# One head's first attention pass alternated with another head's second pass

## The chip, the cores and the metric

The kernel runs on one core of a Trainium2 chip. The metric is the device time of one execution in microseconds (us). The core has five engines with queues of their own: TensorE (PE, matmuls), VectorE (DVE), ScalarE (ACT), GpSimd (POOL) and SyncE (SP, which here only issues DMAs). Each engine takes its instructions in the order that was fixed when the program was compiled.

## The reference

One layer of a hybrid encoder over 2048 positions with 1024 channels, in float32. Cut to what matters here:

```python
def forgetting_attention(q, k, v, f_logit):           # 8 heads of 64, blocks of 128 queries
    c = jnp.cumsum(jax.nn.log_sigmoid(f_logit), axis=1)
    s = jnp.einsum('bhtd,bshd->bhts', qi, k) * Dh ** -0.5
    s = s + ci[..., :, None] - c[:, :, None, :]
    s = jnp.where(kpos[None, :] <= qpos[:, None], s, -jnp.inf)
    p = jax.nn.softmax(s, axis=-1)
    return jnp.einsum('bhts,bshd->bthd', p, v)

h = rms_norm(x, norm_mix_g);  z = h @ w_in
out_a = spatial_gating(gelu(u), gelu(v), ...)         # 8 gating heads
out_b = forgetting_attention(q, k, v, f)              # 8 attention heads
x = x + concat(out_a, out_b) @ w_out
x = x + conv_ffn(rms_norm(x, norm_ffn_g), w_up, w_conv, b_conv, w_down)
return rms_norm(x, norm_final_g)
```

The feed-forward part projects up to 2 x 2816 channels, applies a causal convolution of width 3, a SiLU gate, and projects down.

## The kernel before

**Main work.** The 2048 positions are taken in two halves of 1024, and each half in two token blocks of 512. A float32 matmul is made of three matmuls on rounded high and low parts: `mm3` (L206 to L214; the matmul itself is L212) does so for the projections. `a_half` does the input projections and the gating heads, `c_half` the output projection of the first half, `d_half` the up-projection and convolution of the first half in 22 slices of 128 channels (`d_up`, four times 24 matmuls of 512 columns per slice), `c_late` the output projection of the second half, and `late_half` the rest. In `d_up` a result leaves PSUM by two ACT operations (L934, L935); DVE then does the halo copies (L936, L937), the taps (L938, L939), the gate (L947) and the product (L950). Weights are loaded raw, cast to a high part on POOL (L151), and the low part is made on DVE (L165). In every second slice `d_sums` combines rows of the down-projection on POOL (L992).

**Attention.** A piece is one head and one block `tb` of 512 queries; there are 32, eight heads for each of the four blocks. A piece has two passes over its `tb + 1` blocks of 512 keys:

- `b_max`, the first pass, finds for each query the largest score: for a key block and 128 queries, one matmul into a score bank (L777) and one DVE reduction (L780, or L782 with the causal mask). That is one unit; a piece with `tb` = 3 has 16.
- `b_mix`, the second pass, takes 128 keys a unit: two matmuls for the transposed scores (L824, L828; L826 adds the mask), `Exp` on ACT (L830), a rounded copy on ACT (L835), the low part on DVE (L836), the running sum of the weights on DVE (L838), and, three units later, two matmuls with the values into the output bank (L812, L813). At its end the sums are turned (L854) and, for each pair of heads, the result is scaled and written to the DRAM tensors `mixh` and `mixl`.

The row maxima of the first pass go into rows 96 to 104 of the piece's query tile `t1` by `turn()` (L796, L797).

**Tiles.** `b_keys` (L743) loads key tiles: `m1` (136 KB, wanted by both passes), and for the second pass `m2` and the values `v`. `self.M1` is a ring of two `m1` tiles whose constant rows are set once (L702); both passes take turns in it. `t1` has two buffers, the second query tile `t2` (loaded by `b_low`) and the sum tile `sum` have one each. Behind the first two slices of `d_half`, `self.more` is set and the pool `bxpool` is opened: `room` (L729) then takes tiles `e`, `ph`, `pl`, `m2`, `v` from additional buffers too (names with a `+`), and `scores` (L736) takes two banks named `dn` beside the three named `s`.

**Order.** `b_stream` (L708) yields once per unit. `tick` calls one step of it for every `rate` main matmuls (3.6 in `d_half` and `c_late`). The program so traced is ordered for each engine at compile time by priority: earlier in the program first, with the steps of the stream set 100 instructions ahead (`AHEAD_B`) and weight preparation 2000 (`AHEAD_W`). An instruction that isn't ready is passed by those behind it. `need(n)` finishes the stream up to block `n` at points where its result is read: `c_late` needs block 3 behind its first column of the first token block, and then loads `mixh` and `mixl` of that block (`load_mix`, L872) for its second token block.

In `b_stream` the first pass of a piece runs in full, then the second pass of the piece before it:

Of the kernel before, what the change touches and what calls it, by code (L numbers as in the profile page):

```python
# [8 lines left out]
F32 = mybir.dt.float32  # L9
F32R = mybir.dt.float32r  # L10
# [8 lines left out]
P = 128  # L19
# [6 lines left out]
TB = 512  # L26
# [7 lines left out]
AHEAD_B, AHEAD_W = 100, 2000  # L34
WARM = 24
LAG = 2
TURN = 3
GATE_LAG = 30

# [14 lines left out]
def f32(ap):  # L54
    return ap.bitcast(F32)
# [26 lines left out]
class Block:  # L82
# [625 lines left out]
    def b_stream(self, pieces):  # L708

        todo = None  # L710
        for h, tb in pieces:
            if tb >= 2 and not self.ready:
                if todo:
                    yield from self.b_mix(*todo, None)
                    self.done += 1
                    todo = None
                while not self.ready:
                    yield
            t1, turn = yield from self.b_max(h, tb)
            if todo:  # L720
                yield from self.b_mix(*todo, turn)
                self.done += 1
            else:
                turn()
            todo = (h, tb, t1, self.b_low(h, tb))
        yield from self.b_mix(*todo, None)
        self.done += 1

    def room(self, shape, dt, tag):  # L729

        n = self.nroom[tag] = self.nroom.get(tag, -1) + 1
        if self.more and n % (BUFS[tag] + BUFS[tag + "+"]) >= BUFS[tag]:
            return self.til(self.bx, shape, dt, tag + "+")
        return self.til(self.bp if tag == "e" else self.mp, shape, dt, tag)
# [7 lines left out]

    def b_keys(self, h, sb, values):  # L743
        hf, sl = sb // 2, slice((sb % 2) * TB, (sb % 2 + 1) * TB)
        self.M1.append(self.M1.pop(0))
        m1 = self.M1[0]
        self.dma(f32(m1[0:68, :]), self.kx[hf][h, 64:132, sl])
        if not values:
            return m1
        m2 = self.room([P, TB], F32R, "m2")  # L750
        self.dma(f32(m2), self.kx[hf][h, 0:128, sl])
        v = self.room([P, 4, P], F32R, "v")
        self.dma(f32(v), self.vd[hf][sl, h, :].rearrange("(c p) d -> p c d", p=P))
        return m1, m2, v

    def b_low(self, h, tb):

        t2 = self.til(self.mp, [P, TB], F32R, "t2")
        self.dma(f32(t2), self.qx[tb // 2][h, :, (tb % 2) * TB:(tb % 2 + 1) * TB])
        return t2  # L760

# [37 lines left out]

        return t1, turn  # L800

    def b_mix(self, h, tb, t1, t2, turn):

        nc, bp, pp = self.nc, self.bp, self.bpp
        po = self.til(pp, [P, TB], F32, "o")
        total = self.til(self.mp, [P, TB], F32, "sum")
        ns = 4 * tb + 4
        late = []

        def pv():  # L810
            sc, c, v, ph, pl = late.pop(0)
            nc.tensor.matmul(po[:, c], lhsT=v, rhs=ph[:, c], start=sc == 0, stop=False)  # L812
            nc.tensor.matmul(po[:, c], lhsT=v, rhs=pl[:, c], start=False, stop=sc == ns - 1)  # L813

        for sc in range(ns):
            if sc == TURN and turn:
                turn()
            if sc % 4 == 0:
                m1, m2, v4 = self.b_keys(h, sc // 4, True)
            j = max(0, sc - 4 * tb)  # L820
            c = slice(j * P, TB)
            ks = slice((sc % 4) * P, (sc % 4 + 1) * P)
            ps = self.scores([P, TB])
            nc.tensor.matmul(ps[:, c], lhsT=m1[:, ks], rhs=t1[:, c], start=True, stop=False)  # L824
            if sc >= 4 * tb:
                nc.tensor.matmul(ps[:, j * P:(j + 1) * P], lhsT=self.same, rhs=self.maskT, start=False, stop=False,  # L826
                                 skip_group_check=True)
            nc.tensor.matmul(ps[:, c], lhsT=m2[:, ks], rhs=t2[:, c], start=False, stop=True)  # L828
            e = self.room([P, TB], F32, "e") if sc else total
            nc.scalar.activation(e[:, c], ps[:, c], AF.Exp, scale=-1.0)  # L830
            if len(late) >= (LAG + 1 if self.more else LAG):
                pv()
            ph = self.room([P, TB], F32R, "ph")
            pl = self.room([P, TB], F32R, "pl")
            nc.scalar.activation(ph[:, c], e[:, c], AF.Copy)  # L835
            nc.vector.tensor_tensor(pl[:, c], e[:, c], f32(ph[:, c]), op=ALU.subtract)  # L836
            if sc:
                nc.vector.tensor_tensor(total[:, c], total[:, c], e[:, c], op=ALU.add)  # L838
            late.append((sc, c, v4[:, sc % 4, :], ph, pl))
            yield  # L840
        while late:
            pv()
            yield

        if h % 2 == 0:
            self.op = self.til(self.mp, [P, TB], F32, "op")
            self.rr = self.til(bp, [P, 4, 2], F32, "rr")
        op = self.op
        own, other = (slice(0, 64), slice(64, 128)) if h % 2 == 0 else (slice(64, 128), slice(0, 64))
        nc.scalar.activation(op[own, :], po[other, :], AF.Copy)  # L850
        nc.vector.tensor_tensor(op[own, :], po[own, :], op[own, :], op=ALU.add)
        ps = self.scores([P, 4])
        for i in range(4):
            nc.tensor.matmul(ps[:, i:i + 1], lhsT=total[:, i * P:(i + 1) * P], rhs=self.mhalf[:, 0:1], start=True, stop=True)  # L854
        nc.vector.reciprocal(self.rr[:, :, h % 2], ps)
        if h % 2 == 0:
            return

        rw = self.til(self.mp, [P, 4, 2, 64], F32, "rw")
        nc.scalar.activation(rw, self.rr.unsqueeze(3).broadcast_to([P, 4, 2, 64]), AF.Copy, scale=-0.5)  # L860
        yield
        pr = self.transpose4(None, "s", [rw[:, i, :, :].rearrange("p a b -> p (a b)") for i in range(4)])
        nc.vector.tensor_tensor(op, pr, op, op=ALU.mult)
        oh = self.room([P, TB], F32R, "ph")
        ol = self.room([P, TB], F32R, "pl")
        self.split_sb(op, oh, ol)
        cs = slice(512 + (h - 1) * 64, 512 + (h + 1) * 64)
        self.dma(self.mixh[tb][cs, :], f32(oh))
        self.dma(self.mixl[tb][cs, :], f32(ol))
# [84 lines left out]
    def d_half(self):  # L954

        units = lambda f: [self.load_unit(self.a["w_up"][c], P) for c in (f, NF + f)]
        for f0 in range(0, NF, 2):
# [17 lines left out]
            if not f0:  # L975
                self.flush()
                self.accs.close()
                self.bx = self.bxs.enter_context(self.tc.tile_pool(name="bxpool", bufs=1, side="right", reuse_waits="tile"))
                self.more = True
    def d_sums(self, i):  # L980

        nc, dp = self.nc, self.dp
# [579 lines left out]
```

## Time and profile before

| | |
|---|---|
| median of three runs | 2421.57 us (2420.01 to 2422.13) |
| the profiled execution's own time | 2422.66 us |
| its span in the trace | 2420.9 us |
| granted PE clock, mean | 0.995 |
| first unit that uses the additional score banks | 967.5 us |
| last value matmul of attention (L813) | 1512.5 us |

How to read it: busy times are unions of an engine's instructions. Matmuls are pipelined, so that one of 512 columns is shown as 390 ns long while the next starts 226 ns behind it; the pace of PE is read from starts and counts, not from durations. In rows of waits and timelines, "<-" names what ended the wait. Tile names stand without buffer numbers, so `m` is `m1` or `m2`, and `t` is `t1` or `t2`, or the convolution's `t`.

### The profile page before, as it was taken

How to read it: one execution, taken by the hardware profiler on the slowest of the kernel's cores; microseconds unless marked ns; L12 is line 12 of the kernel's file. 1: busy time of each engine (PE TensorE's matmuls, PEld its weight loads, DVE VectorE, ACT ScalarE, POOL GpSimd, SP SyncE). 2: the span in 40 equal slices, each digit the busy share in tenths (PEclk: the TensorE clock that was granted, in tenths of full speed). 3: DMA queues.
4: the chain of work that ended last, by engine and by line, in shares of the span. 5: the costliest groups of instructions: out<-in, count | busy, mean ns of one | idle time of the engine just before them, and what ended most of it. 6: DMA issues, size and time to landing. Idle time of an engine off the chain costs nothing.

```text
span 2420.9 us, 32633 instructions
## 1 busy us (share of the span) xinstructions
PE 2379.3 (98%) x11352; PEld 1973.2 (82%) x11352; DVE 1881.9 (78%) x3196; ACT 1152.9 (48%) x1987; POOL 331.3 (14%) x315
## 2 busy tenths in 40 slices
PE   9999999999999999999999999899999999999998
PEld 7888878988787888888878888688888888888887
DVE  5457776776579888998999988598888877857775
ACT  4335655533334444454544445465555455454444
POOL 4014140010232222222221110100000000000001
PEclk9999999999999999999999999899999999999999
DMA  8662625567754444444443464312222228438633
GB/s 278 184 230 94 197 74 171 153 188 247 244 193 151 154 142 153 147 140 158 160 155 121 159 217 152 122 53 95 79 81 85 87 93 313 159 98 296 205 119 123
DMA packets 234518, 379.58 MB, mean 157 GB/s; under 512 B 49944, under 2 KB 109464, under 8 KB 232928
## 3 DMA queue, kind: packets, MB, share of 16 engines
q1 hardware_dynamic: 229312, 353.36, 44.9%
q0 software_dynamic: 5040, 24.12, 2.6%
q8 instruction: 90, 1.47, 0.3%
q14 instruction: 76, 0.62, 0.1%
HBM read 283.82 MB, written 93.72 MB: 156 GB/s over the span
## 4 chain that ended last, share of the span: by engine, by line
PE 79%; DVE 5%; DMA 2%; issue 2%; ACT 2%; POOL 1%; SPq 0%; POOLq 0%; DVEq 0%; ACTq 0%
PE mm L212 35%; PE D L1376 13%; PE A L1174 3%; PE A L1176 3%; PE A L1175 3%; PE o L813 3%; PE o L812 2%; PE s L777 2%; PE s L828 2%; PE s L824 2%; PE B L1175 2%; PE B L1176 2%; PE B L1174 2%; PE C L1174 1%; PE C L1175 1%
## 5 line engine op out<-in xcount | busy, mean ns | idle before, releaser
L212 PE MATMUL mm<-thi,wlo 128*128 128x512 f32 x896 | 352.9, 394 | 0.0
L212 PE MATMUL mm<-thi,whi 128*128 128x512 f32 x896 | 352.1, 393 | 0.5 <-DVE vn L520 0.5
L212 PE MATMUL mm<-tlo,whi 128*128 128x512 f32 x896 | 352.5, 393 | 0.0
L212 PE MATMUL mm<-whi,thi 128*128 128x512 f32 (+2 forms) x768 | 277.4, 362 | 14.3 <-DMA thi<-mixh 8.8
L212 PE MATMUL mm<-wlo,thi 128*128 128x512 f32 (+2 forms) x768 | 276.7, 361 | 1.9 <-DVE wlo L165 1.8
L212 PE MATMUL mm<-whi,tlo 128*128 128x512 f32 (+2 forms) x768 | 275.4, 360 | 1.3 <-DMA tlo<-mixl 1.3
L151 POOL TENSOR_SCALAR whi<-raw 128x1024 fp32r<-128x1024 f32 (+3 forms) x114 | 135.2, 1187 | 909.3 <-PE mm L212 665.9
L212 PEld LDWEIGHTS mm<-thi,whi 128*128 128x128 f32 x896 | 168.8, 188 | 34.5 <-issue 0.9
L212 PEld LDWEIGHTS mm<-tlo,whi 128*128 128x128 f32 x896 | 168.8, 188 | 33.9
L212 PEld LDWEIGHTS mm<-thi,wlo 128*128 128x128 f32 x896 | 168.9, 188 | 33.2
L838 DVE TENSOR_TENSOR sum<-sum,e 128x512 f32<-128x512 f32 (+3 forms) x249 | 163.6, 657 | 20.8 <-ACT e L830 18.2
L212 PEld LDWEIGHTS mm<-whi,thi 128*128 128x128 f32 x768 | 146.1, 190 | 35.8 <-DMA thi<-mixh 9.6
L212 PEld LDWEIGHTS mm<-wlo,thi 128*128 128x128 f32 x768 | 146.1, 190 | 22.5 <-DVE wlo L165 3.1
L212 PEld LDWEIGHTS mm<-whi,tlo 128*128 128x128 f32 x768 | 146.0, 190 | 21.4 <-DMA tlo<-mixl 1.7
L830 ACT ACTIVATE e<-s 128x512 f32<-128x512 f32 (+3 forms) x207 | 105.9, 518 | 114.0 <-PE s L828 64.1
L165 DVE TENSOR_TENSOR wlo<-raw,whi 128x1024 fp32r<-128x1024 f32 (+2 forms) x106 | 134.8, 1274 | 28.0 <-POOL whi L151 27.6
L1376 PE MATMUL D<-wh,xh 128*128 128x512 f32 x368 | 140.8, 389 | 1.2 <-DVE xo L1477 1.2
L1376 PE MATMUL D<-wl,xh 128*128 128x512 f32 x368 | 141.4, 389 | 0.0
L836 DVE TENSOR_TENSOR pl<-e,ph 128x512 fp32r<-128x512 f32 (+3 forms) x195 | 122.2, 632 | 20.5 <-PE o L813 10.7
L1376 PE MATMUL D<-wh,xl 128*128 128x512 f32 x368 | 137.5, 389 | 0.0
L835 ACT ACTIVATE ph<-e 128x512 fp32r<-128x512 f32 (+3 forms) x195 | 104.4, 547 | 42.4 <-PE o L812 29.5
L934 ACT ACTIVATE a<-mm 128x512 f32<-128x512 f32 x88 | 52.4, 596 | 119.5 <-PE mm L212 119.1
(1839 smaller groups left out, 5776.2 us busy)
## 6 DMA issues: line engine op xcount, KB each, us to landing
raw<-in_w_up_dram SPq DMA_DIRECT2D x72, 512.0 KB
m<-kx SPq DMA_DIRECT2D x160, 136.0 KB
x<-act SPq DMA_DIRECT2D x84, 256.0 KB
m<-kx SPq DMA_DIRECT2D x67, 256.0 KB
v<-vd SPq DMA_DIRECT2D x67, 256.0 KB
raw<-in_w_in_dram SPq DMA_DIRECT2D x28, 512.0 KB
raw<-in_w_out_dram SPq DMA_DIRECT2D x24, 512.0 KB
tw<-in_w_down_dram SPq DMA_DIRECT2D x11, 1024.0 KB
```

The costliest lines, as they stand in the source:

```text
L151: self.cast_ins = self.nc.gpsimd.tensor_scalar(out, in_, 1.0, 0.0, ALU.mult, ALU.add).ins
L165: nc.vector.tensor_tensor(lo, raw, f32(hi), op=ALU.subtract)
L212: self.last_mm = self.nc.tensor.matmul(ps, lhsT=a[k], rhs=b[k], start=i == 0, stop=i == 3 * n - 1).ins
L813: nc.tensor.matmul(po[:, c], lhsT=v, rhs=pl[:, c], start=False, stop=sc == ns - 1)
L830: nc.scalar.activation(e[:, c], ps[:, c], AF.Exp, scale=-1.0)
L835: nc.scalar.activation(ph[:, c], e[:, c], AF.Copy)
L836: nc.vector.tensor_tensor(pl[:, c], e[:, c], f32(ph[:, c]), op=ALU.subtract)
L838: nc.vector.tensor_tensor(total[:, c], total[:, c], e[:, c], op=ALU.add)
L1174: mm(ps, lhsT=xh[:, ks], rhs=yh[:, k, :], start=fresh and k == 0, stop=False, **kw)
L1175: mm(ps, lhsT=xh[:, ks], rhs=yl[:, k, :], start=False, stop=False, **kw)
L1176: mm(ps, lhsT=xl[:, ks], rhs=yh[:, k, :], start=False, stop=k == 3, **kw)
L1376: nc.tensor.matmul(bank[t], lhsT=x[i][:, ts], rhs=w[k], start=fresh and j == 0 and i + k == 0, stop=last and i == 1, **kw)
```

## The change

While `self.more` holds, three units of the new piece's first pass alternate with two units of the second pass of the piece before, until the first pass is done; the rest of the second pass follows, and `turn()` is called behind its fourth unit. The second pass gets a ring of its own of two key tiles, `self.M1b`, whose constant rows are set by four memsets on POOL when `bxpool` is opened. `t2` and `sum` get a second buffer each, and `t2` is loaded at the start of the second pass, not at the end of the round before.

```diff
+FIRST, SECOND = 3, 2
...
-    ... "m2+": 1, "v+": 1,
+    ... "m2+": 1, "v+": 1, "m1+": 2, "sum+": 1, "t2+": 1,
...
-            t1, turn = yield from self.b_max(h, tb)
-            if todo:
-                yield from self.b_mix(*todo, turn)
+            if todo and self.more:
+                first, second = self.b_max(h, tb), self.b_mix(*todo, None)
+                t1 = None
+                while t1 is None:
+                    for _ in range(FIRST):
+                        t1, turn = yield from self.one(first)
+                        if t1 is not None:
+                            break
+                    if t1 is None:
+                        for _ in range(SECOND):
+                            yield from self.one(second)
+                for n, _ in enumerate(second):
+                    if n == TURN:
+                        turn()
+                        turn = None
+                    yield
+                if turn:
+                    turn()
                 self.done += 1
             else:
-                turn()
-            todo = (h, tb, t1, self.b_low(h, tb))
+                t1, turn = yield from self.b_max(h, tb)
+                if todo:
+                    yield from self.b_mix(*todo, turn)
+                    self.done += 1
+                else:
+                    turn()
+            todo = (h, tb, t1)
...
+    def one(self, gen):
+        try:
+            next(gen)
+        except StopIteration as end:
+            return end.value or (None, None)
+        yield
+        return None, None
...
     def b_keys(self, h, sb, values):
-        self.M1.append(self.M1.pop(0))
-        m1 = self.M1[0]
+        ring = self.M1b if values and self.more else self.M1
+        ring.append(ring.pop(0))
+        m1 = ring[0]
...
     def b_low(self, h, tb):
-        t2 = self.til(self.mp, [P, TB], F32R, "t2")
+        t2 = self.room([P, TB], F32R, "t2")
...
-    def b_mix(self, h, tb, t1, t2, turn):
+    def b_mix(self, h, tb, t1, turn):
+        t2 = self.b_low(h, tb)
         po = self.til(pp, [P, TB], F32, "o")
-        total = self.til(self.mp, [P, TB], F32, "sum")
+        total = self.room([P, TB], F32, "sum")
...
                 self.more = True
+                self.M1b = [self.til(self.bx, [P, TB], F32R, "m1+") for _ in range(2)]
+                for m in self.M1b:
+                    self.nc.gpsimd.memset(f32(m[64:128, :]), 0.0)
+                    self.nc.gpsimd.memset(f32(m[96:104, :]), 1.0)
```

2 rows, old and new, of the table BUFS are left out of this document.

## The prediction, as it stood before the changed kernel was run

> **What bounds the kernel now.** I read the page first, then busy time by stretches, then the waits and the timeline of TensorE (PE), then the groups of VectorE (DVE).
>
> ```profile
> span 2420.9 us, 32633 instructions
> PE 2379.3 (98%) x11352; PEld 1973.2 (82%) x11352; DVE 1881.9 (78%) x3196; ACT 1152.9 (48%) x1987; POOL 331.3 (14%) x315
> ```
>
> PE idles 42 us in all, so a reordering has little to win, and only where PE idles or runs slowly. The next rows are stretches: bounds, length, then busy time (and count) of PE, PEld, DVE, ACT, POOL, the granted clock, DMA share and GB/s; the last row counts only the matmuls of the helper at L212, the feed-forward and projection work that I call main work.
>
> ```profile
> 1700.00:1800.00 100.00, 100.00 (x443) 82.80 (x442) 84.91 (x107) 52.62 (x81) 0.00 (x0) 1.00 0.24 85
> 1099.00:1427.00 328.00, 326.81 (x1509) 267.95 (x1509) 304.28 (x563) 165.29 (x302) 59.26 (x49) 1.00 0.48 158
> 1129.00:1157.00 28.00, 28.00 (x130) 22.83 (x129) 27.37 (x53) 21.02 (x40) 6.61 (x5) 1.00 0.51 171
> 1157.00:1181.00 24.00, 24.00 (x113) 19.95 (x112) 20.53 (x45) 5.52 (x9) 1.61 (x2) 1.00 0.32 102
> 1099.00:1427.00 328.00, 246.66 (x938) 174.72 (x939) 1.00 0.48 158
> ```
>
> Where PE does nothing but 512-wide matmuls it starts one every 100/443 = 0.226 us. In 1099 to 1427, where attention heads run beside the feed-forward, PE is full and DVE is busy 304.28 of 328 us, 93%. The third row is one second pass (27.37 of 28, 98%), the fourth a first pass (20.53 of 24, 86%): the two kinds of stretch load DVE differently, and the change mixes them. From 967, where the second buffer set comes into use, to 1510 PE waited for only two things:
>
> ```profile
> PE o L813 <- DVE pl+_2522_11042 L836: 1.1, 1, 1.1
> PE o L813 <- DVE pl L836: 0.4, 1, 0.4
> ```
>
> So inside the stretch 1.5 us can be won. More lies at its end:
>
> ```profile
> 1510.08 0.39 PE L212 MATMUL mm<-whi,tlo 128*128 128x512 f32 x1
> ...
> 1512.49 0.31 PE L813 MATMUL o<-pl+_3164_13598,v 128*128 128x128 f32 x1
> 1514.13 0.94 PE L186 MATMUL dn<-ident,rw 128*128 128x128 f32 x4 [1.33 <-ACT rw L860]
> 1522.37 0.80 PE L212 MATMUL mm<-whi,thi 128*128 128x512 f32 x1 [7.30 <-DMA thi<-mixh]
> 1522.96 0.63 PE L212 MATMUL mm<-wlo,thi 128*128 128x512 f32 x1
> 1523.39 0.63 PE L212 MATMUL mm<-whi,thi 128*128 128x512 f32 x1
> ...
> 1534.17 0.39 PE L212 MATMUL mm<-wlo,thi 128*128 128x512 f32 x1
> 1534.40 0.39 PE L212 MATMUL mm<-whi,tlo 128*128 128x512 f32 x1
> ```
>
> The last head's values end at 1512.49, when the main work that does not need them has just run out (1510.08). PE then waits 1.33 and 7.30 us for the head's result to go to memory and back, and some 12 matmuls start 0.43 us apart instead of 0.23 (2.4 us); the transposes in between lose about 0.8. This tail costs 8.6 + 2.4 + 0.8, about 12 us. It is there because attention ends late. Counting steps in the source (one per 3.6 main matmuls), the stream of heads is issued in full by the 15th or 16th of the 22 feed-forward slices; on the chip it ends behind all 22 and 192 output-projection matmuls more. So heads run as fast as their own buffers and engines let them, not at the issue rate.
>
> **The change part by part.** Counts first: no matmul, activation or vector operation is added or removed, and the steps per round are the same. A round here is one head's first pass plus another's second. Added are four memsets on POOL for the two key tiles; the same form took
>
> ```profile
> L702 POOL MEMSET m<- x2: 522/524/526, 38.9 to 39.4; 64x512 f32 x2
> ```
>
> so about 2 us on an engine that is busy 18% (59.26 of 328) here. A weight cast queued behind them is hidden by the weight buffers: 0, at most 2 if that cover is gone. The query tile is now loaded at the start of its second pass, not a round ahead, into one of two buffers, so SyncE can issue it while the other is in use; at worst one landing per round would show, and only on that head, whose place main work takes on PE: 0. The second sum tile and key ring change no count of loads. What moves is the pace of the heads. Six rounds now take
>
> ```profile
> 1098.82 0.39 PE L777 MATMUL s<-m,t 96*128 96x512 f32 x1
> ...
> 1426.86 0.40 PE L777 MATMUL dn<-m,t 96*128 96x512 f32 x1
> ...
> 1457.95 0.40 PE L777 MATMUL s<-m,t 96*128 96x512 f32 x1
> ```
>
> 328.0/6 = 54.7 us each. Behind 1457.95 only two second passes are left and they end at 1512.49: 27.3 each, the rest of a round is the first pass. A first pass is slow because its two key tiles are a shared ring:
>
> ```profile
> 1055.34 0.27 SPq L101 DMA_DIRECT2D m<-kx  x1
> ...
> 1062.65 0.40 PE L777 MATMUL s<-m,t 96*128 96x512 f32 x1
> ```
>
> the third key block is asked for at 1055.34, when the first is done, and used 7.3 us later. With its own ring and another head's units in between, this latency no longer holds the heads up; DVE does. Its groups in 1099 to 1427:
>
> ```profile
> L939 DVE SCALAR_TENSOR_TENSOR t<-a,cols,t 128x512 f32<-128x512 f32 x39 | 32.1, 824 | 0.3
> L938 DVE SCALAR_TENSOR_TENSOR t<-a,cols,t 128x512 f32<-128x512 f32 x39 | 29.9, 767 | 1.1 <-ACT t L935 1.0
> L780 DVE TENSOR_REDUCE part<-s 128x1 f32<-128x512 f32 x41 | 27.4, 683 | 1.5 <-PE s L777 1.4
> L165 DVE TENSOR_TENSOR wlo<-raw,whi 128x1024 fp32r<-128x1024 f32 x20 | 25.4, 1272 | 0.0
> L780 DVE TENSOR_REDUCE part<-dn 128x1 f32<-128x512 f32 x31 | 20.9, 684 | 4.4 <-PE dn L777 4.4
> L947 DVE SCALAR_TENSOR_TENSOR t<-a,t 128x512 f32<-128x512 f32 x20 | 16.9, 847 | 3.7 <-ACT a L946 3.6
> L950 DVE TENSOR_TENSOR va<-t,t 128x512 f32<-128x512 f32 x19 | 13.5, 711 | 0.2
> L936 DVE COPY a<-halo 128x2 f32<-128x2 f32 x38 | 11.0, 288 | 0.1
> L937 DVE COPY halo<-a 128x2 f32<-128x2 f32 x39 | 8.2, 209 | 6.5 <-ACT a L934 6.5
> ```
>
> All but L780 is main work: 32.1 + 29.9 + 25.4 + 16.9 + 13.5 + 11.0 + 8.2 = 137 us. It belongs to 938 matmuls, 938 x 0.226 = 212 us of PE: 0.65 us of DVE per us of main PE work, about 0.61 because neighbouring operations overlap at their ends. Heads then take (304 - 0.61 x 212)/6 = 29 us of DVE and (328 - 212)/6 = 19 us of PE in a round. If a round takes R and main gets X of PE, DVE is full at R = 29 + 0.61 X, PE at R = 19 + X: both at X = 25.6, R = 44.6. A slower round leaves PE full. A faster one means that the heads take DVE from the feed-forward, whose two PSUM banks then stay full, and PE idles; that idle time does not come back later, since behind the heads PE is full by itself.
>
> How fast will a round be? Second passes run at 27.3 us where main work gives DVE little, and at 28 among the convolutions, so heads go ahead of main work. Twelve reductions a round (41 + 31 over six) and four masked ones add at least
>
> ```profile
> 1363.09 0.69 DVE L838 TENSOR_TENSOR sum<-sum,e+_2786_12111 128x512 f32<-128x512 f32 x1
> 1363.69 0.69 DVE L836 TENSOR_TENSOR pl<-e,ph 128x512 fp32r<-128x512 f32 x1
> ```
>
> 0.60 us (start to start) each, some 10 us: 37. I add 3 for the start of a round, when the new query tile is awaited: R = 40. The ends: 29 (DVE does nothing else) and 54.7 (no quicker); I stand nearer the low end since a second pass alone was measured at 27.3. At R = 40, X = 11/0.61 = 18, PE is busy 37 and idles 3.0. Alternating rounds are seven of full size and three shorter ones (24, 24 and 28 of 32 units), 9.4 in full ones: 9.4 x 3.0 = 28 us. In return the heads end some 100 us ahead of need, the tail is covered: -12. Sum +16. Against the profiled execution's own 2422.66 us, 1.1 over the median, that is 2438.7, or 2437.6 by the median: 2438.
>
> **The rivals.** *Heads moderately faster, PE stays full.* If shared score banks and DVE keep R between 44.6 and about 53.5, the heads still end 11 us or more ahead, since ten rounds each give a us, and the tail is covered: 2421.6 - 12 = 2410. For it: any speed-up between 2 and 18% will do, and DVE has 24 of 328 us free. Against it: the low pace of second passes alone. The decision lies at R = 44.6. The Trainium skill ("Perfetto Trace Analysis", Optimization Strategy) advises interleaving regimes whose most-contended engine differs, which would speak for this case; the trace shows the different regimes (98% and 86%), but in both of them DVE is high.
>
> *POOL's sums block a fuller DVE.* While POOL forms the down-projection sums, DVE operations that read two SBUF tiles take 1.77 us:
>
> ```profile
> L992 POOL TENSOR_TENSOR tw<-tw 128x512 f32<-128x512 f32 x28 | 44.2, 1580 | 24.5 <-DMA tw<-in_w_down_dram 23.0
> 1255.47 1.77 DVE L836 TENSOR_TENSOR pl+_2522_11042<-e,ph+_2521_11041 128x512 fp32r<-128x512 f32 x1
> 1257.29 0.50 PE L813 MATMUL o<-pl+_2522_11042,v 128*128 128x512 f32 x1 [1.09 <-DVE pl+_2522_11042 L836]
> ```
>
> 28 operations are seven groups of 6.3 us; in one DVE ends about 3.7 operations instead of 10, losing 4 us. Now that costs PE 1.09 us once. With R near 44.6 and no slack, six groups cost up to 4 each, 24 - 12 = +12: 2434. Against it: the heads' buffers may bridge 4 us. The Trainium skill ("SBUF — State Buffer", Who interferes with whom) says the same of a DVE operation with two SBUF inputs against a GpSimd one that reads SBUF: the later blocks fully; here 1.77 beside 1.58 agrees.
>
> *The change does not quicken the heads.* Key loads on one queue, or the single output bank, hold R at 54 or more: tail and stretch stay, 2422, up to 2426 if each round is 0.5 longer.
>
> **How the numbers follow.** Forecast (R from 37 to 42, 2438) 0.40; moderate (2410) 0.35; POOL (2434) 0.12; no quicker (2422) 0.13. What a measurement of this kernel can tell from no change is about 0.2%, 5 us, so faster is 0.35, same 0.13, slower 0.52. The likeliest case alone spans 2427 (R = 42: 1.7 x 9.4 - 12 = +4 and a few us of PE waits that an average hides) to 2460 (R = 36: 5.5 x 9.4 - 12 = +40). The range for 8 in 10 must also hold the moderate case, 12 to 15 below the median: 2407 to 2460.
>
> **What would show it.** Right: L777 and L824 alternate from about 967 on; the last L813 stands well before the feed-forward's last slice, 1350 to 1420; the wait for mixh is gone; PE shows gaps before L212 or L813 ended by DVE or ACT, 20 to 40 us in sum, and DVE is above 97% in the stretch. Wrong: PE still full in the stretch and no wait for mixh (moderate case, faster), or the wait for mixh unchanged (no quicker). The weakest step is R = 40.

## The result, and the profile after

The changed kernel takes 2401.58 us (median of five runs, 2400.57 to 2401.80) against 2421.57 us of the kernel before in the same session (2419.90 to 2423.31): ratio 0.9917, 95% interval 0.9904 to 0.9931. It is 20 us faster; the forecast was 2438 us. The profiled execution has this head in its page (in the sections below, lines of the changed kernel are counted in its own source: L213 is the main matmul, L808 the first pass, L844 and L845 the value matmuls, L868 the low part):

```profile
span 2400.1 us, 32583 instructions
PE 2372.9 (99%) x11352; PEld 1971.3 (82%) x11352; DVE 1863.7 (78%) x3196; ACT 1156.0 (48%) x1985; POOL 329.3 (14%) x319
```

Busy time by stretches, with the columns as before (bounds, length, PE, PEld, DVE, ACT, POOL, clock, DMA share, GB/s):

```profile
967.00:1500.00 533.00, 531.18 (x2475) 435.77 (x2474) 470.12 (x886) 274.17 (x492) 93.42 (x82) 1.00 0.48 161
1099.00:1361.00 262.00, 260.18 (x1210) 212.70 (x1208) 245.61 (x471) 140.08 (x253) 51.29 (x42) 1.00 0.47 156
```

PE is as full as it was (260.18 of 262 us), and DVE hardly fuller: 245.61 of 262 is 93.7%, where 304.28 of 328, 92.8%, stood before. All waits of PE from 900 to 1620 us:

```profile
PE o L845 <- DVE pl L868: 1.7, 3, 0.7
PE tq L187 <- DVE cv L1063: 1.3, 1, 1.3
PE o L845 <- DVE pl+_2538_11100 L868: 0.7, 1, 0.7
PE A L1211 <- ACT t2h L1052: 0.3, 1, 0.3
```

The wait for `mixh` is gone, and no DVE or ACT wait has come in its place. The timeline of PE gives the pace of the heads:

```profile
1063.82 0.70 PE L808 MATMUL s<-m,t 96*128 96x512 f32 x2
...
1361.09 0.70 PE L808 MATMUL dn<-m,t 96*128 96x512 f32 x2
...
1445.75 0.22 PE L845 MATMUL o<-pl+_3166_13604,v 128*128 128x128 f32 x1
1445.81 0.45 PE L213 MATMUL mm<-thi,whi 128*128 128x512 f32 x1
```

These are the first units of the second and the last head of block 3, so six rounds in 297.3 us: 49.5 us a round instead of 54.7. The last value matmul is at 1445.75 instead of 1512.49, and main work follows it at once.

To place the gain I counted PE's lost time: for each matmul the interval to the next start, less the median of that pair of shapes in the kernel before, summed between fixed main matmuls (a count of mine over all matmuls of a trace).

| main matmuls | when, in the kernel before | before | after |
|---|---|---|---|
| 0 to 1800 | to 505 us | 37.4 | 36.3 |
| 1800 to 2300 | 505 to 655 us | 4.3 | 4.6 |
| 2300 to 2800 | 655 to 815 us | 13.6 | 4.7 |
| 2800 to 4800 | 815 to 1493 us, where the alternation runs (from 967) | 18.3 | 21.4 |
| 4800 to 4992 | 1493 to 1566 us, with the tail | 14.1 | 0.2 |
| the rest | | 6.2 | 6.5 |
| sum | | 94.0 | 73.8 |

So 13.9 us came from the tail and 8.9 us from a place where nothing alternates yet. There the kernel before waits (640 to 800 us; the changed kernel has no wait of PE there):

```profile
PE o L813 <- DVE pl L836: 3.8, 2, 2.8
PE mm L212 <- DMA thi<-mixh: 1.5, 1, 1.5
PE mm L212 <- DMA tlo<-mixl: 1.3, 1, 1.3
```

The second and third rows are a small copy of the tail: the output projection of the first half waits for the last head of block 1. Of the whole change, only the moved load of `t2` acts so early.

### The profile page after: what moved, and what is told of

Its sections match the earlier page's. It is cut to its first block, busy times and chain, and to the rows that moved or that the text cites. A ratio compares the mean times of both kernels' runs of the same rounds, so it can differ in the third digit from the quotient of the medians.

```text
span 2400.1 us, 32583 instructions
## 1 busy us (share of the span) xinstructions
PE 2372.9 (99%) x11352; PEld 1971.3 (82%) x11352; DVE 1863.7 (78%) x3196; ACT 1156.0 (48%) x1985; POOL 329.3 (14%) x319
## 4 chain that ended last, share of the span: by engine, by line
PE 83%; DVE 4%; DMA 2%; issue 1%; ACT 1%; POOL 0%; SPq 0%; POOLq 0%; DVEq 0%; ACTq 0%
PE mm L213 37%; PE D L1413 15%; PE A L1211 3%; PE A L1213 3%; PE A L1212 3%; PE o L845 3%; PE o L844 2%; PE s L860 2%; PE s L808 2%; PE s L856 2%; PE B L1213 2%; PE B L1212 2%; PE B L1211 2%; PE C L1211 1%; PE C L1212 1%
## 5 line engine op out<-in xcount | busy, mean ns | idle before, releaser
L213 PE MATMUL mm<-thi,whi 128*128 128x512 f32 x896 | 352.6, 394 | 2.5 <-DVE vn L521 2.5
L213 PE MATMUL mm<-tlo,whi 128*128 128x512 f32 x896 | 353.5, 394 | 0.0
L213 PE MATMUL mm<-thi,wlo 128*128 128x512 f32 x896 | 353.0, 394 | 0.0
L213 PE MATMUL mm<-whi,thi 128*128 128x512 f32 (+2 forms) x768 | 276.6, 361 | 6.1 <-DVE vn L521 5.9
L213 PE MATMUL mm<-wlo,thi 128*128 128x512 f32 (+2 forms) x768 | 275.9, 359 | 1.6 <-DVE wlo L166 1.6
L213 PE MATMUL mm<-whi,tlo 128*128 128x512 f32 (+2 forms) x768 | 275.3, 359 | 0.0
L213 PEld LDWEIGHTS mm<-thi,whi 128*128 128x128 f32 x896 | 169.1, 189 | 36.4 <-issue 2.8
L213 PEld LDWEIGHTS mm<-tlo,whi 128*128 128x128 f32 x896 | 168.9, 189 | 34.1
L213 PEld LDWEIGHTS mm<-thi,wlo 128*128 128x128 f32 x896 | 169.1, 189 | 33.9
L213 PEld LDWEIGHTS mm<-whi,thi 128*128 128x128 f32 x768 | 146.0, 190 | 26.2 <-DVE vn L521 6.1
L213 PEld LDWEIGHTS mm<-wlo,thi 128*128 128x128 f32 x768 | 146.1, 190 | 22.1 <-DVE wlo L166 2.3
L213 PEld LDWEIGHTS mm<-whi,tlo 128*128 128x128 f32 x768 | 145.9, 190 | 19.9
L868 DVE TENSOR_TENSOR pl<-e,ph 128x512 fp32r<-128x512 f32 (+3 forms) x195 | 121.8, 630 | 18.7 <-PE o L845 13.2
L870 DVE TENSOR_TENSOR sum<-sum,e 128x512 f32<-128x512 f32 (+3 forms) x189 | 118.5, 627 | 18.1 <-ACT e L862 14.9
L811 DVE TENSOR_REDUCE part<-s 128x1 f32<-128x512 f32 x140 | 94.2, 683 | 16.2 <-PE s L808 15.6
```

Of the source, the lines that this page charges most:

```text
L213: self.last_mm = self.nc.tensor.matmul(ps, lhsT=a[k], rhs=b[k], start=i == 0, stop=i == 3 * n - 1).ins
L811: nc.vector.tensor_reduce(dst, ps, axis=AX.X, op=ALU.min)
```

## The experiments

Times are medians, compared with runs of the kernel before on the same chip (2420.7 to 2423.6 us in all sessions).

**Taking the change apart.** Four runs. In the first the load of `t2` goes back to its old place, the rest of the change stays:

```diff
-            todo = (h, tb, t1)
+            todo = (h, tb, t1, self.b_low(h, tb))
```

> The changed kernel with one part undone: the load of t2 goes back to the end of the round before, with the two buffers that it has after 967 us; the alternation and the key ring stay. Theory (two separate gains: the load's place is worth 8.9 us of TensorE between 640 and 800 us, the earlier end of the heads 13.9 us behind 1500 us): about 2410 us, with the idle at 663, 667 and 729 us back and no wait for mixh behind 1500 us. Rival (the order of instructions merely fell better, the load's place has nothing to do with it): 2402 us. Second rival (the two-buffer load in the alternating stretch matters as well): above 2414 us.

Measured: 2406.24 us, ratio 0.9931 (0.9919 to 0.9944). Lost time 13.3 us at 655 to 815 us and 0.2 in the tail; 49.2 us a round, heads end at 1462.8. As expected, the early loss is back and the tail stays covered; the time lies midway between the theory (2410) and the first rival (2402). The second run is the other half, the kernel before with nothing but the load moved:

```diff
-            todo = (h, tb, t1, self.b_low(h, tb))
+            todo = (h, tb, t1)
...
+        t2 = self.b_low(h, tb)          # first line of b_mix
```

> The kernel before with one part of the change alone: the load of t2 moved to the start of the second pass; no alternation, no own key ring. Theory (two separate gains): about 2413 us, the idle at 663, 667 and 729 us gone, the wait for mixh behind 1500 us as before. Rival (the load's place is worth nothing, as the prediction costed it): 2421.5 us. Second rival (the load now comes late for a sequential second pass): above 2423 us and heads that end later than 1512 us.

Measured: 2401.78 us, ratio 0.9912 (0.9897 to 0.9928). That is the whole gain without any alternation, and 11 us more than I expected: rounds of 53.1 us end the heads at 1486.8, and that is early enough for the tail to go too (lost time 4.9 and 0.3 us). So the two gains are not separate: either half covers the tail, and only the load covers 655 to 815 us.

The third takes out the trip through memory at the tail: `load_mix` for block 3 reads block 2's data.

> The kernel before with the last block of mixh and mixl never read: the load for the last token block reads the third block's data instead, so the product behind the heads does not wait for the last head. The heads themselves stay as slow as they are. Theory (the end of the heads cost 12 to 14 us): about 2408 to 2410 us, TensorE with neither the 1.33 and 7.30 us of idle nor the slow matmuls behind 1512 us. Rival (the work of the last heads in the tail is what costs, not the trip through memory): above 2415 us.

Measured: 2421.88 us, ratio 1.0000 (0.9991 to 1.0009). My theory failed. The timelines of PE and of ACT in this run:

```profile
1516.56 0.22 PE L813 MATMUL o<-pl+_3164_13598,v 128*128 128x128 f32 x1
1517.32 0.66 PE L186 MATMUL dn<-ident,rw 128*128 128x128 f32 x4
1525.31 3.93 PE L186 MATMUL dn<-ident,ar 128*128 128x128 f32 x16 [7.34 <-ACT ar L1072]
```

```profile
1519.43 0.63 ACT L199 ACTIVATE ph+_3168_13642<-op 128x512 fp32r<-128x512 f32 x1 [1.56 <-DVE op L863]
1519.97 1.04 ACT L176 ACTIVATE ar<-acc 128x1024 f32<-128x1024 f32 x1
...
1524.12 4.25 ACT L1072 ACTIVATE ar<-acc,rstd 128x1024 f32<-128x1024 f32 x4
```

PE idles 7.34 us as before, now for the scaled rows of the first token block: in ACT's queue their operations (L176, L1072) stand behind the last head's L199. The tail is a place where several queues wait for the last head; taking one wait away uncovers the next. It was gone in every run whose heads ended by 1490.9 us; what else would remove it was not tried.

The fourth leaves the alternation without key tiles of its own:

```diff
-        ring = self.M1b if values and self.more else self.M1
+        ring = self.M1
```

> The changed kernel without key tiles of the second pass's own: both passes take turns on the two tiles of the first ring, as before, still alternating in units. Theory (the alternation needs the ring: a key tile of one pass is asked for while the other pass still reads the other two): rounds of 53 us or more instead of 49.6, heads that end behind 1490 us, about 2407 to 2420 us. Rival (the engines set the round, not the key tiles): 49.6 us a round and 2402 us.

Measured: 2439.5 us, ratio 1.0069 (1.0056 to 1.0081), 60.2 us a round, heads end at 1526.7, lost time 28.9 us in the tail. Worse than my range. Its waits of PE between 970 and 1620 us begin:

```profile
PE mm L213 <- DMA thi<-mixh: 7.9, 1, 7.9
PE s L856 <- DMA m<-kx: 5.6, 3, 2.4
PE dn L808 <- DMA m<-kx: 3.3, 1, 3.3
```

With two tiles for two passes both wait for key loads. The ring is what makes the alternation possible; it is no gain by itself, as the run without alternation shows (`FIRST = 99`, the first pass in one turn, all else of the change kept):

> The changed kernel with 99 units of the first pass in a turn instead of 3, so the first pass runs in full before the second begins: the key ring, the second sum and t2 tiles and the load's new place stay, the alternation goes. Theory (the alternation quickens the round, the ring alone does not; but the time does not depend on the round any more once the heads end before 1500 us): rounds of 52 to 54 us, attention ends at 1475 to 1490 us, 2402 us. Rival (the key ring quickens the round, not the alternation): rounds of 49 to 50 us, 2402 us. Second rival (the alternation is worth time by itself): 2406 us or more.

Measured: 2402.14 us, ratio 0.9913 (0.9898 to 0.9928), 54.2 us a round, heads end at 1490.7, the last two just outside what I had put down. So the alternation shortens a round from 54.2 to 49.5 us, and this buys no time that can be told: 2402.14 against 2401.58 us, and the intervals of the two ratios overlap.

**What sets the round, and who gives way.** Three changed kernels. Without the running sum on DVE:

```diff
+            lean = self.more if sc == 0 else lean
+            if sc == 0 and lean:
+                nc.vector.tensor_scalar(total, total, 1.0, None, ALU.add)
-            if sc:
+            if sc and not lean:
                 nc.vector.tensor_tensor(total[:, c], total[:, c], e[:, c], op=ALU.add)
```

> The changed kernel without the running sum of the weights on VectorE while the units alternate (each head's sum is that of its first key tile plus one, so the weights are scaled wrongly): 15 operations of 0.6 us, 9 us of VectorE a round, are taken out. Theory (VectorE, 94% busy there, sets the round of 49.6 us): rounds of 44 us or less, TensorE still full, 2400 to 2402 us, since nothing that TensorE waits for is left. Rival (key loads, score banks or the order of the instructions set the round): 48.5 us or more a round, VectorE at some 80%, 2402 us.

Measured: 2400.92 us, ratio 0.9905 (0.9890 to 0.9919), 44.4 us a round, heads end at 1395.6, and a stretch of

```profile
1099.00:1361.00 262.00, 260.31 (x1210) 212.21 (x1209) 214.92 (x409) 148.24 (x271) 41.49 (x36) 1.00 0.47 152
```

Of 9 us of DVE work taken out of a round, its length gives back 5.1 (44.4 us, where I had said 44 or less), though DVE is then busy only 82%. So these operations are a large part of what holds the round, not all of it. Whether by DVE's time or as a link of the head's own chain, which releases the `e` tiles, this run doesn't part. With key and value loads on GpSimd's queue (`self.nc.gpsimd.dma_start` in `b_keys` while `self.more`):

> The changed kernel with the key and value loads of both passes issued from GpSimd's queue instead of SyncE's while the units alternate; nothing else moves. Theory (a key load stands in SyncE's queue behind others that wait, and this is a part of the round): rounds shorter than 48 us; if they come below 44.6 us, the prediction's step says that TensorE begins to idle and the time passes 2405 us. Rival (VectorE sets the round): 49 to 50 us and 2402 us. Second rival (GpSimd, now held by waiting loads, casts weights late): TensorE waits for the high parts of the weights, 2410 us or more.

Measured: 2403.88 us, ratio 0.9920 (0.9905 to 0.9934), 49.5 us a round: key loads in SyncE's queue do not hold the alternating round. The third puts 16 operations more on DVE:

```diff
-            nc.vector.tensor_tensor(pl[:, c], e[:, c], f32(ph[:, c]), op=ALU.subtract)
+            for _ in range(2 if self.more else 1):
+                nc.vector.tensor_tensor(pl[:, c], e[:, c], f32(ph[:, c]), op=ALU.subtract)
```

> The changed kernel with the low part of the weights computed twice on VectorE while the units alternate: 16 more operations of 0.6 us a round, 9.6 us. It tests the step of the prediction by which heads take VectorE ahead of the main work. By that step: the round stays at 50 to 52 us and main work goes short, (50 - 38.6) / 0.61 = 18.7 us of TensorE for main and 12 us idle in a round of 50, over 9.4 rounds some 110 us: about 2510 us. Theory (main work keeps its share and the heads give way): rounds of 54 to 60 us, TensorE full from 967 to 1490 us, and nothing lost until the heads end behind 1500 us: 2402 to 2415 us.

Measured: 2452.97 us, ratio 1.0126 (1.0110 to 1.0141), 62.7 us a round. Stretches, and the timeline of PE at its end:

```profile
1099.00:1361.00 262.00, 257.97 (x1167) 207.83 (x1167) 261.20 (x477) 119.76 (x217) 62.25 (x44) 1.00 0.42 140
```

```profile
1543.41 0.45 PE L845 MATMUL o<-pl+_3166_13768,v 128*128 128x128 f32 x1
...
1546.15 1.12 PE L187 MATMUL dn<-ident,rw 128*128 128x128 f32 x4 [1.53 <-ACT rw L893]
1554.32 0.80 PE L213 MATMUL mm<-whi,thi 128*128 128x512 f32 x1 [7.05 <-DMA thi<-mixh]
1554.91 0.63 PE L213 MATMUL mm<-wlo,thi 128*128 128x512 f32 x1
```

DVE is full (261.20 of 262 us), and PE still works 257.97 of them. The prediction's step, with heads that keep their pace, asked for 12 us of idle PE in each round, 50 us in this stretch; it is 4. Even at the measured round its balance (38.6 us of DVE for the heads, 0.61 for main work) gives 4.2 us of idle PE a round, 18 us in the stretch. The heads gave way: they end at 1543.41, and then the loss comes at once, 49.4 us in the tail (I had expected rounds of 54 to 60 us and a loss of at most 14). In this kernel it is mainly the heads that give way; how late they would be I had underrated.

**Why the load's place is worth anything.** SyncE issues in order. At the change of rounds in the kernel before, its timeline and PE's:

```profile
1204.41 1.08 SPq L101 DMA_DIRECT2D t<-qx  x2
1205.54 0.28 SPq L101 DMA_DIRECT2D t<-cc  x1
1205.87 0.26 SPq L101 DMA_DIRECT2D m<-kx  x1
```

```profile
1204.16 0.22 PE L824 MATMUL s<-t,m 128*128 128x128 f32 x1
...
1211.67 0.71 PE L777 MATMUL s<-m,t 96*128 96x512 f32 x2
```

and with the load moved:

```profile
1176.11 0.45 SPq L101 DMA_DIRECT2D t<-qx  x1
1176.61 0.44 SPq L101 DMA_DIRECT2D t<-cc  x1
1177.14 0.26 SPq L101 DMA_DIRECT2D m<-kx  x1
1177.45 0.34 SPq L101 DMA_DIRECT2D t<-qx  x1
```

```profile
1175.86 0.22 PE L825 MATMUL s<-t,m 128*128 128x128 f32 x1
...
1184.48 0.48 PE L777 MATMUL s<-m,t 96*128 96x512 f32 x1
```

Both query loads wait for the last unit of the running second pass (1204.16, 1175.86). Before, `t2`, wanted a whole first pass later, is issued ahead of `t1`, `cc` and the first key tile, which the next first pass waits for. Moved, it stands behind them. From the start of the last second-pass unit to the issue of `cc` the median over 30 rounds is 1.43 us before and 0.79 us with the load moved. At the change of rounds shown, the first unit itself does not come sooner for it (7.5 us behind the last unit before, 8.6 with the load moved); over 30 rounds the median of that distance is 8.10 us before and 6.94 with the load moved.

To 30 rounds 0.64 us each is 19 us, and the heads ended 25.7 us earlier. But these 25.7 us are not spread evenly: 9.6 are there when block 2 starts, 13.7 come in its first two rounds (649 to 740 us before), and 2.4 in all the rest. In the second of these rounds SyncE stands, in the kernel before, 5.1 us before a weight load, whose buffer a low part on DVE still reads (L165), and the query loads stand behind it (timeline of SyncE, and its waits from 715 to 735 us):

```profile
722.30 0.33 SPq L101 DMA_DIRECT2D acc<-in_x_dram  x1
727.78 0.33 SPq L101 DMA_DIRECT2D raw<-in_w_up_dram  x1
728.17 1.08 SPq L101 DMA_DIRECT2D t<-qx  x2
729.29 0.29 SPq L101 DMA_DIRECT2D t<-cc  x1
```

```profile
SPq L101 <- DVE wlo L165: 6.8, 2, 5.1
```

So `cc` is issued 5.4 us behind the last unit there, and the round takes 60.6 us, where it takes 49.2 with the load moved. More than the issue time of one load is at work. The first of two runs on this puts the load behind the first unit of the first pass instead:

```diff
+            first = self.b_max(h, tb)
+            next(first)
+            if todo:
+                todo += (self.b_low(*todo[:2]),)
+            yield
+            t1, turn = yield from first
```

> The kernel before, sequential passes, one t2 buffer; t2 is loaded neither at the end of the round before nor at the start of the second pass, but behind the first unit of the first pass, so behind that pass's own query and key loads in SyncE's queue. Theory (in its old place the t2 load, which waits for the last unit of the running second pass, stands in the queue ahead of the loads of the next first pass and holds them up; any place behind them gains): 2401 to 2405 us, as with the load at the start of the second pass. Rival (that gain was one lucky order of the instructions, and another small shift of the load gives another result): 2408 us or more.

Measured: 2399.5 us, ratio 0.9901 (0.9885 to 0.9918), `cc` again 0.79 us behind the unit: the gain that the theory asks for, and 1.5 us more than my range. The second doubles the cost in the old place, with two loads of 64 partitions:

> The kernel before with the load of t2 in its old place, ahead of the next first pass's loads, but cut into two loads of 64 partitions: one more issue of some 0.55 us on SyncE in each round, the suspected cost doubled. Theory (the heads are one chain from round to round, and what stands in SyncE's queue ahead of the next first pass's loads is paid in every round): the first pass starts 0.5 to 0.9 us later in each of 30 rounds, the heads end 15 to 27 us later, at 1528 to 1540 us, and as TensorE waits for them there the time grows by as much: 2435 to 2450 us. Rival (the load's place gained in another way, not through SyncE's queue): 2420 to 2425 us.

Measured: 2412.17 us, ratio 0.9952 (0.9937 to 0.9967): faster, where I had said 13 us slower or more. The lag is what it should be, 2.07 us, but the compiler had ordered all queues otherwise, and that order was better elsewhere (5.4 us lost at 655 to 815 us against 13.6). So the kernel before and the kernel after differ in an order as well as in a place, and one comparison can't part them. Six more runs try to: both places under the same small disturbances, and a larger dose. With halves in the new place:

> The kernel before with the load of t2 at the start of the second pass, and in two halves: the partner of the run with halves in the old place (2412 us). Theory (the place gains by itself, some 0.7 us of each round): 2398 to 2404 us, heads that end 15 us or more before the 1504 us of that run. Rival (only the order of the instructions differs, drawn anew with each edit): anything from 2400 to 2422 us, as likely above 2412 us as below.

The heads' priority 85 instead of 100 (`AHEAD_B`), old and new place:

> The kernel before with the heads' steps set 85 instead of 100 instructions ahead, the load of t2 in its old place: another order, nothing else. Theory of the place: 2415 to 2426 us, as every order with the old place pays for it. Rival (the kernel before had a poor order): 2400 to 2412 us.

> The same with the load of t2 at the start of the second pass. Theory of the place: 2398 to 2404 us. Rival (order alone): anything from 2400 to 2422 us.

Value loads in two halves, old and new place:

> The kernel before with each load of values cut into two, one more issue on SyncE per key block; the load of t2 in its old place. Theory of the place: 2412 us or more, as all orders with the old place. Rival (the kernel before had a poor order): 2400 to 2412 us.

> The same with the load of t2 at the start of the second pass. Theory of the place: at least 8 us below its partner with the old place, 2398 to 2408 us. Rival (order alone): as likely above its partner as below.

And four loads of 32 partitions in the old place:

> The kernel before with the load of t2 in its old place cut into four loads of 32 partitions, three issues more of about 0.5 us each ahead of the next first pass's loads. Theory (each issue there is paid in every round): the first pass starts 1 us later than with halves, in each of 30 rounds, so heads that end some 30 us later than the 1504 us of the run with halves, and 2435 us or more. Rival (order alone): 2400 to 2422 us, with heads that end before 1515 us.

Measured, all with sequential passes; lag is that of `cc`, the last two columns are lost time of PE in us, at 655 to 815 us and in the tail:

| | time | ratio (95%) | lag | heads end | 655 to 815 | tail |
|---|---|---|---|---|---|---|
| old, as before | 2421.6 | 1 | 1.43 | 1512.5 | 13.6 | 14.1 |
| old, priority 85 | 2418.4 | 0.9985 (0.9975 to 0.9994) | 1.48 | 1508.0 | 11.8 | 14.0 |
| old, value halves | 2419.1 | 0.9993 (0.9984 to 1.0003) | 1.42 | 1508.5 | 11.1 | 15.3 |
| old, halves | 2412.2 | 0.9952 (0.9937 to 0.9967) | 2.07 | 1504.0 | 5.4 | 8.5 |
| old, quarters | 2430.8 | 1.0042 (1.0027 to 1.0057) | 2.80 | 1519.4 | 13.5 | 15.6 |
| new | 2401.8 | 0.9912 (0.9897 to 0.9928) | 0.79 | 1486.8 | 4.9 | 0.3 |
| new, priority 85 | 2405.4 | 0.9931 (0.9916 to 0.9946) | 0.78 | 1490.9 | 4.9 | 0.4 |
| new, value halves | 2408.9 | 0.9951 (0.9937 to 0.9966) | 0.80 | 1498.3 | 4.8 | 8.6 |
| new, halves | 2410.8 | 0.9955 (0.9940 to 0.9970) | 0.77 | 1503.6 | 5.8 | 9.3 |

By the medians the new place is faster by 20, 13, 10 and 1 us, 11 in the mean. Three of the four pairs show it; the pair of halves, run in two sessions, does not: its ratios, 0.9952 with the old place and 0.9955 with the new one, are the same within their intervals. Values from 1 to 20 leave the mean of four uncertain by about 12 us at 95%. The lag follows the number of issues ahead (0.64 us for each of the first two, 2.01 for four); with quarters, SyncE's issues at one change of rounds, grouped (count, shortest, median and longest duration in ns, first and last start), are the four loads of `t2` and the one of `t1`, and then `cc`:

```profile
L101 SPq DMA_DIRECT2D t<-qx x5: 412/419/575, 1211.0 to 1213.0; - x5
L101 SPq DMA_DIRECT2D t<-cc x1: 281/281/281, 1213.5 to 1213.5; - x1
```

But the end of the heads does not follow the lag: two halves in the old place end at 1504.0, a whole load at 1512.5, and two halves in the new place, with a lag 1.3 us shorter, at 1503.6, where I had expected 15 us or more. And several of my ranges were missed: halves in the new place (2410.8, outside 2398 to 2404), priority 85 and value halves in the new place by 1 us each, and quarters (2430.8, below 2435), which ended 15 us later than halves, not 30. So the place probably gains, and an edit that changes the order moves the time by up to 9 us besides: down with the old place (2421.6 to 2412.2), up with the new one (2401.8 to 2410.8). The pair of this change is the one with the largest difference: a part of its 20 us is probably the luck of its order, and how much can't be said. One part of the luck can be read off. The second round of block 2 takes 60.6, 61.2, 61.2 and 62.0 us with the old place (as before, priority 85, value halves, quarters), 50.9 us with halves in the old place, and 49.2 us in all four kernels with the new one. Whether the place makes the difference there, or the order that comes with it, I did not settle.

**The waits at 663 us alone.** The kernel before, with `load_mix` for block 1 reading block 0's data:

> The kernel before with the load for the second token block of the first half's output projection taking the first block's data, so that TensorE does not wait there for the last head of block 1 (the idle of 1.5 and 1.3 us at 663 to 667 us). Theory (of the 8.9 us that the changed kernel saved between 640 and 800 us, these waits are 2.8, and the rest is the meeting of a head's low parts with GpSimd's sums at 729 us, which fell elsewhere): 2418 to 2420 us. Rival (all of it follows from that wait): 2413 us. Second rival (as in the tail, other work in the queues waits for the head all the same): 2421.5 us.

Measured: 2416.6 us, ratio 0.9976 (0.9966 to 0.9985), between theory and first rival. The 2.8 us of waits are gone, and the lost time there falls from 13.6 to 8.5 us. But this run doesn't part those waits from the meeting of a low part with GpSimd's sums at 729 us: its queues are ordered otherwise too, and that meeting is gone as well (PE waits four times for a low part from 640 to 800 us, 2.3 us in all and 0.8 at most). What the meeting is, the timelines of GpSimd, DVE and PE in the kernel before show:

```profile
725.38 3.50 POOL L992 TENSOR_TENSOR tw<-tw 128x512 f32<-128x512 f32 x2
```

```profile
727.68 1.74 DVE L836 TENSOR_TENSOR pl<-e,ph 128x512 fp32r<-128x512 f32 x1
...
729.42 0.68 DVE L836 TENSOR_TENSOR pl<-e,ph 128x512 fp32r<-128x512 f32 x1
```

```profile
729.48 0.80 PE L813 MATMUL o<-pl,v 128*128 128x512 f32 x1 [2.80 <-DVE pl L836]
730.07 0.63 PE L812 MATMUL o<-ph,v 128*128 128x512 f32 x1
```

The low part took 1.74 us beside the sums and 0.68 behind them, and PE waited 2.80 us. The Trainium skill ("SBUF — State Buffer", Who interferes with whom) says that these two engines share one pair of ports which one of them holds alone at a time; the trace agrees.

**Both together.** The alternating kernel with `t2` loaded as in the 2399.5 us kernel while the passes are sequential:

> The changed kernel, alternating, with t2 loaded behind the first unit of the next first pass while the passes are still sequential, as in the sequential kernel that took 2399.5 us. Theory (the place in SyncE's queue gives all of the gain, the alternation adds nothing to it as the heads end in time either way): 2399 to 2402 us. Rival (alternation and place add up): below 2397 us.

Measured: 2398.27 us, ratio 0.9899 (0.9884 to 0.9914), heads end at 1443.7. The lowest median of all, and just below my 2399 to 2402, but its interval overlaps those of the sequential kernels with the load moved (0.9901 and 0.9912) and of the changed kernel (0.9917): the alternation adds nothing that these runs can tell.

## Why the prediction was wrong

It said 2438 us, slower; the time is 2401.58, below its range (2407 to 2460). Two terms of its sum failed: R = 40, with the +28 us of idle PE that hung on it (measured: R = 49.5 and +3), and the 0 for the moved load (8.9 us of PE at 655 to 815 us alone). The sum was +28 - 12 + 0 = +16; by the lost time of PE it came to +3.1 - 13.9 - 8.9 = -19.7.

- *PE is full in the stretch, the loss lies in the tail* (right). The tail was put at 12 us and gave 13.9. Its mechanism was told too narrowly: the trip through memory was named as the wait, and taking out the trip alone gave nothing, since ACT's queue waits for the last head as well. With later heads the price rises: 0.4 us at 1490.9, 8.5 at 1504.0, 14.1 at 1512.5, 28.9 at 1526.7, 49.4 at 1543.4.
- *The moved load of `t2`: 0* (wrong). The step asked whether the load might come late, not what it stood ahead of in SyncE's queue. Alone it gives 20 us here; in four pairs it gives 1 to 20, 11 in the mean. In the prediction's sum, where the tail is taken off already, its share is the 8.9 us at 655 to 815: with them the forecast would still have been 7 us slower. I also read the waits of PE only from 967 us on; three rows at 640 to 800 us hold 6.6 us, 2.8 of them of the same kind as the tail.
- *R = 40* (wrong). It was a second pass alone, 27.3, plus twelve reductions and four masked ones, 10, plus 3. Measured 49.5, and heads that end at 1445.75, not at 1350 to 1420. A second pass that alternates with the other pass did not keep the pace that it has by itself. Nor does the second pass's own key ring quicken the round: with the ring and without alternation it takes 54.2 us, so it was not the sharing of the two tiles that made a first pass slow in sequence.
- *Heads go ahead of main work on DVE, so that PE idles 3.0 us a round, +28* (wrong, and the step that made the forecast slower). The alternating stretch lost 21.4 us of PE against 18.3, +3. With R at 49.5 the prediction's own balance has PE full, so here the size of R alone undoes the +28. The order of precedence was tested apart: with DVE at 99.7%, in the run with doubled low parts, PE idled 4 of 262 us. That second passes ran at 27.3 us with and 28 without convolutions had been my only evidence, and it doesn't show who gives way when DVE is full. R itself never came under 44.6 in a kernel with all its DVE work, so what would happen there was not seen.
- *The memsets: 0* (not tested by themselves; PE shows no wait for a weight cast, and the run with all of the change but the alternation took the time of the load's move alone).
- The rival *heads moderately faster, PE stays full* (0.35, 2410 us) was the case: R between 44.6 and 53.5, tail covered. Its time is 8 us off, which is the lost time at 655 to 815 us, 8.9. *POOL's sums block a fuller DVE*: +3 us in the stretch at most. *Not quickened*: no, but it would have cost nothing with the load moved.
- The Trainium skill's advice ("Perfetto Trace Analysis", Optimization Strategy) to interleave regimes held for the round, 54.2 to 49.5 us, and not for the time: PE was full in both regimes.

## What to carry to other kernels

A chain that runs beside full main work is worth quickening only up to the point where its result is needed; look for every such point (here two, at 663 and 1512 us), and read each as a price over the chain's end, not as one wait to be removed. On a queue that issues in order, ask of each load what it stands ahead of, and what it stands behind: here a load that was wanted late and issued early held the next loads up by 0.64 us at a change of rounds, and a weight load that waited for its buffer held them up by 5 us at one. And where the compiler orders the queues, a single comparison mixes an edit with a new order: repeat both sides under a few small disturbances before putting a number on the edit.

## What the runs showed of the hardware

I had not expected that DVE could run at 99.7% over 262 us (261.20 busy) while PE stays at 98.5% (257.97): in that run the full engine slowed the heads (62.7 us a round for 49.5) and hardly the main work. Issues on SyncE that wait for nothing between them stand about 0.5 us apart, so that a load cut into four took from 1211.0 to the `cc` load at 1213.5. And after an idle stretch of only 2.80 us at 729 us PE's next 512-column matmuls stood 0.43 us apart instead of 0.23 for some 3 us, as after the 7 us of the tail.
